# A down projection as seven products over pairs of row blocks, its operands' sums made earlier, its results added by accumulating transfers

## The chip, the cores and the metric

The kernel runs on one NeuronCore of a Trainium2 chip. The core has five engines with instruction queues of their own: TensorE (PE in the profile, with PEld for its weight loads), VectorE (DVE), ScalarE (ACT), GpSimd (POOL) and SyncE (SP), which here does nothing but issue transfers. Each queue runs in order, and queues wait for each other through semaphores. The metric is the device time of one launch in microseconds (us), the median of several runs.

## What is computed

One step of a hybrid encoder layer (a state space branch and a differential attention branch, then a convolutional feed-forward part) on 1088 tokens: 1024 of a prompt and 64 of running streams. The change lies in the last part of it:

```python
D_MODEL, D_FF, FFN_CONV = 1024, 2816, 3
    x = x + mix @ p['w_out']
    h = _rmsnorm(x, p['norm_ffn_w']) @ p['w_up']          # 1024 -> 2 * 2816
    ha, hb = jnp.split(h, 2, axis=-1)
    hc, ffn_new = _causal_dwconv(ffn_past, ha, p['ffn_conv_w'], p['ffn_conv_b'])
    x = x + (jax.nn.silu(hc) * hb) @ p['w_down']          # 2816 -> 1024
    return x, k, v, ssm_new, conv_new, ffn_new
```

## The kernel before

Activations are kept transposed: features on the 128 partitions, the 1088 tokens along the free axis. Everything is float32; a product is made of operands split into a high and a low half of the type fp32r (`hi` is ScalarE's rounded copy, `lo` is VectorE's difference), and three matmuls stand for one: hi*hi, hi*lo, lo*hi. A *split* below is this pair of instructions, the cast on ScalarE and the subtraction on VectorE.

The last two stages are the *way up* (`w_up`) and the *way down* (`w_down`).

**The way up** (`pair`, lines 970 to 1041 of the kernel before) takes 22 steps, here called pairs. One pair makes two row blocks of 128 features, block `f` of `ha` and block `f` of `hb`, over all tokens by a seven-product scheme of the Strassen-Winograd kind: the weights of the two blocks are cut in quarters (K halves by row blocks), the activations in quarters (K halves by token halves), and seven products of sums of quarters replace eight. Token quarters are 272 wide (`QW`), `s` is 0 or 1 for the two quarters of a half, and `p` counts the seven parts. One `(p, s)` is a *pile*: 4 tiles of K by 3 terms, 12 matmuls of 128x128 by 272 into a PSUM bank. So a pair is 14 piles, 168 matmuls. Seven banks go round; `a`, `b`, `c`, `d` are the accumulations of a pair, and `a`, `b`, `c` are read out once (an *evacuation*) and then added to further: p = 0 and 2 share `a`, p = 1 and 3 share `b`, p = 4 and 6 share `c`. So a pile of p = 6 can begin only when the evacuation of p = 4, same `s`, is done.

The right operands, `B[part, s]`, are made once ahead of the way up and live in units of SBUF (`home`). The left operands (`left_parts`, line 907) are made anew for each pair, one pair ahead: two transfers of the weights, four sums on GpSimd (lines 917, 918, 928, 935) and seven splits (lines 841, 842). When a pair's results are out, `gate` runs the convolution (two instructions on ScalarE and two on VectorE, line 1003, for each token half), GpSimd multiplies (line 1009) and SP stores the block to `h_sc` in DRAM (line 1010). The work for the second token half of a pair ends in the next pair.

**The way down** (lines 1080 to 1101) is a plain product. `hidden_row` reads a block of 128 rows of `h_sc` back (tile `hr`) and splits it into the units that the way up has left. The 22 blocks of K come in three groups of 8, 6 and 8 (`DOWN`). For each group and each of 8 blocks of output rows, the weights are loaded and split, then for token pieces of 384, 384 and 320 the running sum is loaded from DRAM (`xa`), a product of 3 times 8 (or 6) matmuls is made, VectorE adds the PSUM bank to `xa` (line 1097) and SP stores it (line 1098). The running sum goes through `x1_sc`, `x2_sc` and `x3_sc` to the output `yT`.

The order of each queue is set at build time by a list scheduler that goes by program order, priorities and its own timeline; it is the same in every run.

Of the kernel before, what the change touches and what calls it, by code (L numbers as in the profile page):

```python
# [17 lines left out]
P = 128  # L18
# [14 lines left out]
DOWN = (8, 6, 8)  # L33
# [42 lines left out]
def hybrid_layer(ctx: ExitStack, tc: tile.TileContext, xT, prm, cst, rope, wvd, win, wbs, wba, wout, wup, wdn,  # L76
# [773 lines left out]
    def output(m, quarters):  # L850
# [3 lines left out]
        for q in quarters:  # L854
# [10 lines left out]
            load(out=x1_sc[P * m : P * (m + 1), cs], in_=x)  # L865
# [42 lines left out]
    def left_parts(f):  # L908

        a = []  # L910
        for r in range(2):
            w = wp.tile([P, WMAX], F32, name="w_f", tag="w_f", bufs=2)
            load(out=w[:, :1024], in_=wup[f + r * FT])
            a += [w[:, :512], w[:, 512:1024]]
        q11, q12, q21, q22 = a
        s1, s2 = (row("fs", n)[:, :512] for n in ("ws1", "ws2"))
# [3 lines left out]
        def own(src):  # L920
            hi, lo = (row("fa", n, R32)[:, :512] for n in ("wh", "wl"))
            split(hi, lo, src)
            return hi, lo
# [6 lines left out]
        t = [wp.tile([P, WMAX], R32, name=n, tag=n, bufs=2) for n in ("w_hi", "w_lo")]  # L930
        for i, src in enumerate((s1, q22)):
            hi, lo = (x[:, 512 * i : 512 * i + 512] for x in t)
            split(hi, lo, src)
            yield hi, lo
        G.tensor_tensor(out=s2, in0=q12, in1=s2, op=ALU.subtract)
        hi, lo = (wp.tile([P, WMAX], R32, name=n, tag=n, bufs=2)[:, :512] for n in ("w_hi", "w_lo"))
        split(hi, lo, s2)
        yield hi, lo

# [16 lines left out]
    left = {0: list(left_parts(0))}  # L956
    coming = left_parts(1)
# [8 lines left out]
    def hidden_row(r):  # L966

        name, s = PARTS[r % 14 // 2], r % 2
        hi, lo = (unit(*at) for at in home[name, s])
        for j in range(2):  # L970
            t = couple(row("fb", "hr"))
            load(out=t, in_=h_sc[P * r : P * (r + 1), 2 * QW * j : 2 * QW * (j + 1)].rearrange("p (a t) -> p a t", a=2))
            split(hi[:, 2 * j : 2 * j + 2], lo[:, 2 * j : 2 * j + 2], t)
        return [u.rearrange("p a t -> p (a t)") for u in (hi, lo)]

    def pair(f):
# [6 lines left out]
        banks = {}  # L983

        def pile(key, p, s, start):
            if start:
                banks[key, s] = acc(QW)
            ps, w, b = banks[key, s], left[f][p], B[PARTS[p], s]
            for k in range(4):
                c = slice(P * k, P * (k + 1))  # L990
                for i, (x, y) in enumerate(((0, 0), (0, 1), (1, 0))):
                    PE.matmul(ps, w[x][:, c], b[y][:, k], start=start and k == i == 0, stop=k == 3 and i == 2,  # L992
                              skip_group_check=not start)
            return ps
# [48 lines left out]
    def begun(f):  # L1043
        u = pair(f)
        next(u)
        return u

    def more_left(f):
        x = next(coming, None)
        if x is not None:  # L1050
            left.setdefault(f, []).append(x)

    hid = []
# [16 lines left out]
    for f in range(1, FT):  # L1070
        coming = left_parts(f + 1) if f + 1 < FT else iter(())
        u = pairs[1] if f == 1 else begun(f)
        for p, s in rest[1] if f == 1 else [(p, s) for p in range(7) for s in range(2)]:
            u.send((p, s))
            if s == 1:
                more_left(f + 1)
                if f + 1 == FT and p < 4:
                    hid += [hidden_row(len(hid) + i) for i in range(2)]
        if f + 1 < FT:
            left.setdefault(f + 1, []).extend(coming)  # L1080
        del left[f]
    load(out=ffn, in_=ffn_o)


    k0, path = 0, (x1_sc, x2_sc, x3_sc, yT)
    for g, n in enumerate(DOWN):
# [121 lines left out]
```

## Time and profile before

| | |
|---|---|
| time, median of 3 runs | 2528.1 us (2526.99 to 2531.24) |
| span of the profiled execution, first to last instruction | 2526.9 us |
| TensorE busy | 2463.0 us, 97% of the span |
| VectorE, ScalarE, GpSimd busy | 60%, 45%, 21% |
| way up, steady part (21 pairs) | 1819.1 to 2240.2 us |
| last pair of the way up | 2240.2 to 2261.3 us |
| way down | 2261.3 us to the end |

The profile has no time of its own for the profiled execution beside its span; the median of the runs lies 1.2 us above that span. TensorE's busy time is a sum over stages, so what a change of one stage is worth is read in the windows of that stage. Columns of a window row are busy time and number of instructions of PE, PEld, DVE, ACT and POOL, the granted clock, the busy share of the transfer engines and what they moved. In a row of the timeline stand the start, the duration, the engine, the line and operation, and in brackets the idle time before it with what ended it. In a row of instruction groups stand the count, the busy time and the mean duration of one, then the idle time of the engine just before them.

### The profile page before, as it was taken

The page shows a single profiled execution, that of the slowest core. Times are in us where ns is not written, and L with a number is a line of the kernel's source. Part 1 is how long each engine was busy: PE and PEld are TensorE (multiplying, and loading weights), DVE is VectorE, ACT ScalarE, POOL GpSimd, SP SyncE. Part 2 cuts the span into 40 slices and gives each one's busy share as a digit, 9 for nine tenths or more (in the row PEclk, how much of TensorE's full clock was granted, in tenths as well). Part 3 has the DMA queues.
Part 4 walks back from the last instruction along what each step waited for, and adds up shares of the span by engine and source line. Part 5 has one row for each costly group of instructions (what it writes and reads, how often), then busy time and mean ns, then how long its engine had stood idle before and what let it go on. Part 6 is the DMA issues. An engine that isn't in the chain of part 4 may idle for free.

```text
span 2526.9 us, 43448 instructions
## 1 busy us (share of the span) xinstructions
PE 2463.0 (97%) x16646; PEld 2385.1 (94%) x16646; DVE 1507.9 (60%) x2597; ACT 1130.1 (45%) x2426; POOL 522.8 (21%) x584
## 2 busy tenths in 40 slices
PE   8999999999999999999999998999699999999999
PEld 8999999999999999998889898998699999999999
DVE  7326255855787677447667764645876666673422
ACT  6234343644666455357655654225443333341200
POOL 3000000100111001014333230014465555530000
PEclk9999999999999999999999999999799999999999
DMA  5217258545354344255697735663122222256553
GB/s 164 77 55 272 77 202 261 153 143 158 108 150 138 112 144 118 87 198 177 204 350 233 231 126 201 189 203 109 39 82 78 77 77 78 76 193 211 174 159 112
DMA packets 248336, 378.75 MB, mean 150 GB/s; under 512 B 31776, under 2 KB 188320, under 8 KB 248000
## 3 DMA queue, kind: packets, MB, share of 16 engines
q1 hardware_dynamic: 248128, 375.97, 46.6%
q8 instruction: 131, 2.15, 0.4%
q14 instruction: 77, 0.63, 0.1%
HBM read 254.58 MB, written 121.30 MB: 149 GB/s over the span
## 4 chain that ended last, share of the span: by engine, by line
PE 71%; DMA 4%; DVE 3%; ACT 2%; issue 1%; SPq 1%; POOL 0%; ACTq 0%; DVEq 0%; POOLq 0%
PE mx L992 12%; PE mm L149 10%; PE mm L151 10%; PE mm L150 10%; PE mm L992 5%; PE mx L151 4%; PE mx L149 4%; PE mx L150 4%; PE po L583 3%; PE sc L536 1%; PE sc L535 1%; PE pt L564 1%; PE yi L698 1%; PE ye L704 1%; DMA bc<-a_sc 1%; PE stp L710 1%
## 5 line engine op out<-in xcount | busy, mean ns | idle before, releaser
L149 PE MATMUL mm<-xn_hi,w_hi 128*128 128x384 f32 (+1 forms) x1416 | 469.8, 332 | 0.9 <-DVE zr L431 0.9
L151 PE MATMUL mm<-xn_hi,w_lo 128*128 128x384 f32 (+1 forms) x1416 | 467.7, 330 | 0.4 <-DVE w_lo L143 0.4
L150 PE MATMUL mm<-xn_lo,w_hi 128*128 128x384 f32 (+1 forms) x1416 | 466.5, 329 | 0.0
L142 ACT CAST w_hi<-w_f 128x1024 fp32r<-128x1024 f32 (+2 forms) x144 | 149.3, 1037 | 308.1 <-PE mx L150 162.2
L149 PEld LDWEIGHTS mm<-xn_hi,w_hi 128*128 128x128 f32 x1416 | 266.2, 188 | 5.3 <-issue 2.0
L151 PEld LDWEIGHTS mm<-xn_hi,w_lo 128*128 128x128 f32 x1416 | 266.1, 188 | 2.9 <-issue 0.8
L150 PEld LDWEIGHTS mm<-xn_lo,w_hi 128*128 128x128 f32 x1416 | 266.2, 188 | 1.8 <-issue 0.6
L143 DVE TENSOR_TENSOR w_lo<-w_f,w_hi 128x1024 fp32r<-128x1024 f32 (+2 forms) x144 | 181.2, 1259 | 133.4 <-ACT w_hi L142 133.0
L149 PE MATMUL mm<-b_hi,w_hi 128*128 128x384 f32 (+1 forms) x448 | 148.2, 332 | 7.6 <-DVE b_g L193 4.4
L151 PE MATMUL mm<-b_hi,w_lo 128*128 128x384 f32 (+1 forms) x448 | 147.0, 328 | 0.0
L150 PE MATMUL mm<-b_lo,w_hi 128*128 128x384 f32 (+1 forms) x448 | 146.9, 328 | 0.0
L992 PE MATMUL mx<-n,wh 128*128 128x272 f32 x752 | 143.4, 289 | 1.4 <-ACT wh L841 1.4
L992 PE MATMUL mx<-m,w_hi 128*128 128x272 f32 x752 | 142.7, 288 | 0.0
L460 DVE SCALAR_TENSOR_TENSOR cc<-pre,par,cc 128x384 f32<-128x384 f32 (+1 forms) x216 | 126.6, 586 | 23.8 <-ACT cc L458 18.7
L549 ACT ACTIVATE p_t<-sc,mx 128x1024 f32<-128x1024 f32 (+5 forms) x144 | 106.1, 739 | 74.6 <-DVE mx L540 37.1
L992 PEld LDWEIGHTS mx<-n,wh 128*128 128x128 f32 x752 | 118.3, 189 | 1.7 <-ACT wh L841 1.7
L992 PEld LDWEIGHTS mx<-m,w_hi 128*128 128x128 f32 x752 | 118.1, 188 | 0.0
L1009 POOL TENSOR_TENSOR hb<-hb,cc 128x544 f32<-128x544 f32 (+2 forms) x66 | 88.4, 1353 | 115.1 <-ACT w_hi L841 95.0
L151 PE MATMUL mx<-m,w_lo 128*128 128x272 f32 (+2 forms) x366 | 111.9, 307 | 0.0
L150 PE MATMUL mx<-m,w_hi 128*128 128x272 f32 (+2 forms) x366 | 111.9, 306 | 0.0
L149 PE MATMUL mx<-m,w_hi 128*128 128x272 f32 (+2 forms) x366 | 111.8, 306 | 0.0
L992 PE MATMUL mx<-m,w_lo 128*128 128x272 f32 x376 | 108.4, 288 | 0.0
(339 smaller groups left out, 6595.4 us busy)
## 6 DMA issues: line engine op xcount, KB each, us to landing
w_f<-in_win_dram SPq DMA_DIRECT2D x76, 512.0 KB, 3.8
w_f<-in_wup_dram SPq DMA_DIRECT2D x44, 512.0 KB, 3.5
bc<-a_sc SPq DMA_DIRECT2D x32, 512.0 KB, 6.1
h_sc<-hb SPq DMA_DIRECT2D x44, 272.0 KB, 2.1
hr<-h_sc SPq DMA_DIRECT2D x44, 272.0 KB, 5.2
x_sc<-cc SPq DMA_DIRECT2D x48, 192.0 KB, 2.2
xa<-x_sc SPq DMA_DIRECT2D x48, 192.0 KB, 2.5
kh_t<-k_st SPq DMA_DIRECT2D x32, 272.0 KB, 7.5
```

What stands on the lines that cost most here:

```text
L142: S.copy(hi, w)
L143: V.tensor_tensor(out=lo, in0=w, in1=hi, op=ALU.subtract)
L149: PE.matmul(ps, a_hi, b_hi, start=i == 0, stop=False)
L150: PE.matmul(ps, a_hi, b_lo, start=False, stop=False)
L151: PE.matmul(ps, a_lo, b_hi, start=False, stop=i == n - 1)
L460: V.scalar_tensor_tensor(cc[:, :m], pre[:, i : i + m], cw(i), cc[:, :m], ALU.mult, ALU.add)
L535: PE.matmul(ps[:n, a : a + b], lhs, r_hi, start=True, stop=False)
L536: PE.matmul(ps[:n, a : a + b], lhs, r_lo, start=False, stop=True)
L549: act(p_t[:n, :nk], sc[c][:n, :nk], AF.Exp, bias=mx[:n, c : c + 1], accum_out=dst)
L583: PE.matmul(po[:n, :P], a_t[b // 4][:kw, b % 4 * P : b % 4 * P + n], rhs, start=b == 0, stop=b == nb - 1)
L992: PE.matmul(ps, w[x][:, c], b[y][:, k], start=start and k == i == 0, stop=k == 3 and i == 2, skip_group_check=not start)
L1009: G.tensor_tensor(out=hb[h][:, o : o + n], in0=hb[h][:, o : o + n], in1=cc[:, d : d + n], op=ALU.mult)
```

## The change

The way down becomes 12 further steps of the kind of the way up. K is in groups of 8, 8 and 6 row blocks; a group is cut in two halves of 4, 4 and 3 tiles (even and odd row blocks). Within a group, four steps (`pair_down`) each make two blocks of 128 output rows over all tokens by the seven products: 14 piles of 12 matmuls in the first two groups, of 9 in the third. Its left operands go through `left_parts` with blocks of `w_down`, packed anew on the host.

The right operands need sums of quarters of the hidden rows. They are made during the way up: in every second pair, from pair 2 on, `hidden_sums` reads the two row blocks stored last (four transfers into `g` tiles of the ring `fb`), makes the four sums t1 to t4 on GpSimd, and stores them to a new scratch `t_sc` (four transfers). In the last step ahead of each group, `hidden_part` runs after each part p: it loads the part's operand from `h_sc` or `t_sc` (four `hr` tiles a part, 28 a group) into the units that this p has just set free, and splits them; of the four subtractions one goes to GpSimd.

The running sum in DRAM goes. The way up's input `x1` is stored to the output `yT` itself, and each of the four quarter results of a step (128 x 544) is added to `yT` by a transfer that GpSimd issues with an accumulating write, 48 of them in all. There are no `xa` tiles.

```diff
-DOWN = (8, 6, 8)
+DOWN = (8, 8, 6)
...
-    x1_sc, x2_sc, x3_sc = (scratch(n, [D, T]) for n in ("x1_sc", "x2_sc", "x3_sc"))
     h_sc = scratch("h_sc", [DFF, T])
+    t_sc = scratch("t_sc", [4 * DFF // 2, T // 2])
...
-            load(out=x1_sc[P * m : P * (m + 1), cs], in_=x)
+            load(out=yT[P * m : P * (m + 1), cs], in_=x)
...
+    DOWN_AT = [sum(DOWN[:g]) for g in range(len(DOWN))]
+    work = [(None, f) for f in range(FT)] + [(g, j) for g in range(len(DOWN)) for j in range(4)]
+
+    def left_of(i):
+        g, f = work[i]
+        if g is None:
+            return left_parts([wup[f], wup[f + FT]])
+        n, o = P * DOWN[g], 1024 * DOWN_AT[g]
+        return left_parts([wdn[:, o + n * m : o + n * (m + 1)] for m in (2 * f, 2 * f + 1)])
...
+    def hidden_sums(i):
+
+        b11, b12, b21, b22 = (row("fb", n)[:, :HALF] for n in ("g11", "g12", "g21", "g22"))
+        e = row("fb", "ge")[:, :HALF]
+        for u, (x, y) in enumerate(((b11, b12), (b21, b22))):
+            for v, t in enumerate((x, y)):
+                load(out=t, in_=h3[:, 2 * i + u, HALF * v : HALF * (v + 1)])
+        G.tensor_tensor(out=e, in0=b12, in1=b11, op=ALU.subtract)
+        G.tensor_tensor(out=b12, in0=b22, in1=b12, op=ALU.subtract)
+        G.tensor_tensor(out=b11, in0=b22, in1=e, op=ALU.subtract)
+        G.tensor_tensor(out=b21, in0=b21, in1=b11, op=ALU.subtract)
+        for n, t in zip(KIND, (e, b11, b12, b21)):
+            load(out=t3[:, KIND.index(n), i], in_=t)
+
+    def hidden_part(g, name):
+
+        i0, nk = DOWN_AT[g] // 2, DOWN[g] // 2
+        for s in range(2):
+            hi, lo = B[name, s] = [unit(*at) for at in home[name, s]]
+            for j in range(0, nk, 2):
+                n = min(2, nk - j)
+                t = couple(row("fb", "hr"))[:, :n]
...
+                load(out=t, in_=src)
+                S.copy(hi[:, j : j + n], t)
+                (G if s and j else V).tensor_tensor(out=lo[:, j : j + n], in0=t, in1=hi[:, j : j + n], op=ALU.subtract)
...
+    def pair_down(g, j):
...
+        def put(m, h, t):
+            G.dma_start(out=yT[P * m : P * (m + 1), HALF * h : HALF * (h + 1)], in_=t, accum_op=ALU.add)
...
+            if p == 0:
+                S.copy(u1[:, s], pile("a", p, s, True))
+            elif p == 1:
+                V.tensor_tensor(out=u2[:, s], in0=pile("b", p, s, True), in1=u1[:, s], op=ALU.add)
+            elif p == 2:
+                S.copy(c[p][:, qs], pile("a", p, s, False))
+            elif p == 3:
+                V.tensor_tensor(out=u1[:, s], in0=pile("b", p, s, False), in1=u1[:, s], op=ALU.add)
+            elif p == 4:
+                V.tensor_tensor(out=c[p][:, qs], in0=pile("c", p, s, True), in1=u1[:, s], op=ALU.add)
...
+            if s == 1 and p in (2, 4, 5, 6):
+                m, h = {2: (0, 0), 4: (1, 1), 5: (1, 0), 6: (0, 1)}[p]
+                put(2 * j + m, h, c[p])
...
+    for i, (g, f) in enumerate(work[1:], 1):
+        coming = left_of(i + 1) if i + 1 < len(work) else iter(())
+        u = pairs[1] if i == 1 else begun(i)
+        last = i + 1 < len(work) and work[i + 1][0] not in (g, None)
+        for p, s in rest[1] if i == 1 else [(p, s) for p in range(7) for s in range(2)]:
+            u.send((p, s))
+            if s == 1:
+                more_left(i + 1)
+                if last:
+                    hidden_part(work[i + 1][0], PARTS[p])
+                if p == 3 and i < FT + 2 and i % 2 == 0:
+                    hidden_sums(i // 2 - 1)
```

Up to the way up the queues read as before, row for row, but for the target of the `x1` stores. In the way up, TensorE, VectorE and ScalarE keep their order as well; what is new there stands on GpSimd and SP. Three places of the build's order follow.

GpSimd in one pair of the way up, before: behind the sums of the weights (`ws`, `w_f`) and the two small copies comes the multiplication for the first token half.

```order
L1009 TENSOR_TENSOR hb<-hb,cc 128x480
L1009 TENSOR_TENSOR hb<-hb,cc 128x64
L935 TENSOR_TENSOR ws_19395<-w_f,ws_19395 128x512
L1023 COPY pre<-pre 128x2
L982 COPY pre<-par 128x2
L1009 TENSOR_TENSOR hb<-hb,cc 128x544
L1038 COPY con<-pre 128x2
```

The same place after, in every second pair (the line numbers are those of the changed kernel).

```order
L1051 TENSOR_TENSOR hb<-hb,cc 128x480
L1051 TENSOR_TENSOR hb<-hb,cc 128x64
L936 TENSOR_TENSOR ws_19394<-w_f,ws_19394 128x512
L1065 COPY pre<-pre 128x2
L1035 COPY pre<-par 128x2
L989 TENSOR_TENSOR ge<-g_19501,g_19500 128x544
L990 TENSOR_TENSOR g_19501<-g_19503,g_19501 128x544
L991 TENSOR_TENSOR g_19500<-g_19503,ge 128x544
L992 TENSOR_TENSOR g_19502<-g_19502,g_19500 128x544
L1051 TENSOR_TENSOR hb<-hb,cc 128x544
L1080 COPY con<-pre 128x2
```

The four sums stand between the small copies and the multiplication for the first token half.

VectorE in the last pair of the way up, before: low halves of hidden rows (`n<-hr,n`, `m<-hr,m`, units) between the evacuations `u<-mx` of p = 1 and p = 3 and the convolution (`cc`).

```order
L1019 TENSOR_TENSOR u_24167<-mx,u_24166 128x272
L842 TENSOR_TENSOR n_24209<-hr,n_24208 128x544
L842 TENSOR_TENSOR n_24247<-hr,n_24246 128x544 x2
L842 TENSOR_TENSOR m_24257<-hr,m_24256 128x544
L1026 TENSOR_TENSOR u_24166<-mx,u_24166 128x272
L1003 SCALAR_TENSOR_TENSOR cc<-pre,par,cc 128x544
L842 TENSOR_TENSOR m_24257<-hr,m_24256 128x544
```

The same place after.

```order
L1061 TENSOR_TENSOR u_24335<-mx,u_24334 128x272
L1011 TENSOR_TENSOR n_24389<-hr,n_24388 128x544
L842 TENSOR_TENSOR wl<-ws_24371,wh 128x512
L1011 TENSOR_TENSOR n_24431<-hr,n_24430 128x544 x2
L1011 TENSOR_TENSOR m_24441<-hr,m_24440 128x544
L842 TENSOR_TENSOR wl<-w_f,wh 128x512
L1068 TENSOR_TENSOR u_24334<-mx,u_24334 128x272
L1045 SCALAR_TENSOR_TENSOR cc<-pre,par,cc 128x544
```

Between the same two evacuations now stand the low halves of the next step's weights (`wl`) as well; before, no seven-product step followed this pair.

GpSimd at the same time, after (before, it has only the multiplications and small copies of that pair there): from the last weights' sum of pair 21 to the first accumulating transfer.

```order
L936 TENSOR_TENSOR ws_24371<-w_f,ws_24371 128x512
L1065 COPY pre<-pre 128x2
L1011 TENSOR_TENSOR m_24441<-hr,m_24440 128x544
L1011 TENSOR_TENSOR n_24497<-hr,n_24496 128x544
L1051 TENSOR_TENSOR hb<-hb,cc 128x544
L1011 TENSOR_TENSOR m_24548<-hr,m_24547 128x544
```

```order
L918 TENSOR_TENSOR ws_24758<-w_f 128x512
L1051 TENSOR_TENSOR hb<-hb,cc 128x480
L1051 TENSOR_TENSOR hb<-hb,cc 128x64
L919 TENSOR_TENSOR ws_24759<-ws_24758,w_f 128x512
L929 TENSOR_TENSOR w_f<-w_f 128x512
L1011 TENSOR_TENSOR m_24652<-hr,m_24651 128x544
L1092 DMA out_dram<-down 128x544
L1011 TENSOR_TENSOR m_24714<-hr,m_24713 128x544
```

The subtractions of hidden parts, the sums for the weights of the step after next and the first accumulating transfer now stand in one queue.

More of the change, by code (lines that the diff above doesn't have):

```diff
@@ L929, in left_parts @@
         yield own(q21)
-        t = [wp.tile([P, WMAX], R32, name=n, tag=n, bufs=2) for n in ("w_hi", "w_lo")]
+        t = [wp.tile([P, WMAX], R32, name=name, tag=name, bufs=2) for name in ("w_hi", "w_lo")]
         for i, src in enumerate((s1, q22)):
-            hi, lo = (x[:, 512 * i : 512 * i + 512] for x in t)
+            hi, lo = (x[:, 512 * i : 512 * i + n] for x in t)
             split(hi, lo, src)
@@ L964, in hybrid_layer @@
     ffn_o = tri[:, : 4 * FT].rearrange("p (f c) -> p f c", c=4)
[L966 to L974, printed above, removed]
+    HALF = 2 * QW
@@ L982, in pair @@
         G.tensor_copy(pre[1][:, 482:484], par[:, O_FS + 2 * f : O_FS + 2 * f + 2])
[L983 to L994, printed above, removed]
+        pile = piles(f, 4)
         def gate(h):
```

99 lines of the change are left out of this document (56 added, 43 removed).

## Prediction, made before the changed kernel was run

> **What bounds the kernel now.** I read the head of the page first, then windows around the two stages, then single rows at their borders.
>
> ```profile
> span 2526.9 us, 43448 instructions
> PE 2463.0 (97%) x16646; PEld 2385.1 (94%) x16646; DVE 1507.9 (60%) x2597; ACT 1130.1 (45%) x2426; POOL 522.8 (21%) x584
> ```
>
> TensorE is busy nearly everywhere, so a stage is worth its matmuls unless another engine makes it wait. The windows of the stages that the change touches (way up, a steady pair, last pair, way down), and then the rows at the borders of the way down:
>
> ```profile
> 1819.10:2261.30 442.20, 442.20 (x3528) 442.20 (x3527) 307.44 (x475) 181.52 (x323) 230.30 (x246) 1.00 0.27 90
> 1861.04:1882.11 21.07, 21.07 (x170) 21.07 (x169) 14.58 (x23) 8.28 (x15) 10.98 (x12) 1.00 0.23 79
> 2240.20:2261.30 21.10, 21.10 (x170) 21.10 (x169) 16.74 (x31) 14.55 (x25) 3.74 (x6) 1.00 0.95 333
> 2261.20:2520.00 258.80, 258.11 (x1564) 257.85 (x1563) 86.60 (x130) 41.77 (x56) 4.21 (x5) 1.00 0.53 170
> ...
> 2261.34 0.33 PE L149 MATMUL mm<-n,w_hi 128*128 128x384 f32 x1
> ...
> 2523.28 0.31 PE L151 MATMUL mx<-m,w_lo 128*128 128x320 f32 x1
> ...
> 2523.62 0.49 DVE L1097 TENSOR_TENSOR xa<-xa,mx 128x320 f32<-128x320 f32 x1 [2.96 <-PE mx L151]
> ```
>
> TensorE never stops in either stage, at a granted clock of 1.00. VectorE has 14.6 of 21.1 us of work in a steady pair, GpSimd 11.0. In the way down both are nearly free.
>
> **TensorE's part.** The way up runs 3528 matmuls of 272 columns in 442.2 us, 125.3 ns each (the 288 ns of the group rows overlap). The way down before is 8 row blocks x 3 token pieces x 22 tiles x 3 terms = 1584 matmuls, from 2261.3 to 2523.6, 262.3 us or 165.6 ns each. After, it is four steps of 168, four more of 168 and four of 126: 1848 matmuls of 272 columns. I take the 125.3 ns of the way up, where the same instructions stand: 231.6 us. Gain 30.7 us, if nothing makes TensorE wait. Nothing else of the removed work was on the path: the `xa` loads and stores and the VectorE additions ran beside TensorE (258.1 of 258.8 us busy), all but the last, which is in the tail.
>
> **The port that VectorE and GpSimd share.** What the new steps add is on these two engines, and the rows show that they get in each other's way:
>
> ```profile
> 2216.91 0.69 DVE L842 TENSOR_TENSOR w_lo<-ws,w_hi 128x512 fp32r<-128x512 f32 x1
> 2217.52 1.85 DVE L842 TENSOR_TENSOR w_lo<-w_f,w_hi 128x512 fp32r<-128x512 f32 x1
> ...
> 2216.96 1.85 POOL L1009 TENSOR_TENSOR hb<-hb,cc 128x544 f32<-128x544 f32 x1 [4.66 <-ACT w_hi L841]
> ...
> 2186.82 0.69 DVE L842 TENSOR_TENSOR wl<-w_f,wh 128x512 fp32r<-128x512 f32 x1 [1.23 <-ACT wh L841]
> ...
> 2186.89 1.77 POOL L935 TENSOR_TENSOR ws<-w_f,ws 128x512 f32<-128x512 f32 x1
> ...
> L928 POOL TENSOR_TENSOR w_f<-w_f 128x512 f32<-128x512 f32 x19 | 24.6, 1294 | 0.0
> L1030 DVE TENSOR_TENSOR hb<-mx,u 128x272 f32<-128x272 f32 x29 | 12.8, 442 | 29.7 <-PE mx L992 29.0 <-issue 0.7
> ```
>
> The split of 0.69 us takes 1.85 when GpSimd is in the middle of a multiplication: it ends 0.6 us behind GpSimd's end at 2218.81. The other way round, GpSimd's sum of 1.29 us takes 1.77 when VectorE began first. The evacuations, which read PSUM and one SBUF tile, keep their 0.44 us. So the sums of both engines with two SBUF inputs add up. Net prices: a split of 512 columns 0.61 (2216.91 to 2217.52), and, from the rows below, one of 544 0.66 (three in 1.99), `cc` 0.80 (two in 1.61), GpSimd's 480 and 64 together 1.48; GpSimd's 512 is 1.29, so its 544 is an estimated 1.37 by columns.
>
> ```profile
> 2274.70 1.99 DVE L842 TENSOR_TENSOR m<-hr,m 128x544 fp32r<-128x544 f32 x3
> ...
> 2242.18 1.61 DVE L1003 SCALAR_TENSOR_TENSOR cc<-pre,par,cc 128x546 f32<-128x546 f32 x2 [0.38 <-ACT cc L1001]
> ...
> 2244.57 1.48 POOL L1009 TENSOR_TENSOR hb<-hb,cc 128x480 f32<-128x480 f32 x2 [2.60 <-ACT cc L1004]
> ```
>
> [...]
>
> **First border, way up to group 0.** Of the 28 hidden tiles a group, VectorE subtracts 21 and GpSimd 7. All stand in pair 21 and the step behind it. From the `cc` at 2242.18, 2 us into pair 21, to the last subtraction of the last part (b22), GpSimd's order holds: the sums for two steps less the last of the second (7 x 1.29), 7 x 1.37, the two second-half multiplications (2 x 1.48) and the one of 544 (1.37), 23.0 us. VectorE's holds 21 x 0.66, eight weight splits (8 x 0.61) and six `cc` (4.8): 23.6 us. Together 46.6 us. TensorE needs b22 at p = 6 of step 22, 18 us into it (14 piles in 21.07 us, 1.5 each), so 39 us after pair 21 begins, 37 behind that `cc`. It comes some 10 us late, and already in pair 21 the evacuation of p = 4, which p = 6 needs 4.5 us later, stands behind 11 of the hidden tiles. Bounds: VectorE alone with both pairs' evacuations (23.6 + 20 x 0.44 = 32.4) fits into 37: 0. If the evacuations too come in a row with the rest: 46.6 + 8.8 - 37 = 18. [...]
>
> **Second and third border.** There is no convolution: GpSimd 4 x 1.29 + 7 x 1.37 = 14.8, VectorE 13.9 + 4.9 = 18.8, 33.6 in the 36 us from 3 us into step 25 to the use of b22 in step 26. That fits at the end, not on the way: the evacuation of p = 4 has 11 subtractions, 4 weight splits, 4 evacuations and, at most, four weight sums and four subtractions of GpSimd ahead (7.3 + 2.4 + 1.8 + 10.7 = 22.2 from 1.5 on), while p = 6 wants it at 18: up to 5.7 us late, or 0 if GpSimd's come in later. I take 4. The third border has three tiles instead of four, and I take 1 (0 to 3). ScalarE's 28 casts a border, at 0.65 each (row below), are 18 us in 42, where it has 8.3 in a steady pair: covered.
>
> ```profile
> L841 ACT CAST m<-hr 128x544 fp32r<-128x544 f32 x18 | 11.4, 647 | 7.2 <-DMA hr<-h_sc 6.9
> ...
> h_sc<-hb SPq DMA_DIRECT2D x44, 272.0 KB, 2.1
> hr<-h_sc SPq DMA_DIRECT2D x44, 272.0 KB, 5.2
> ...
> out_dram<-xa SPq DMA_DIRECT2D x16, 192.0 KB, 2.4
> ```
>
> Transfers there: 28 x 272 KB, 7.8 MB, are 23 us at the 333 GB/s of the last pair's window, within 39 us. They too take the place of others: on SP the weights of step 23 stand behind 23 of the 28 loads.
>
> **The sums in the way up.** Four on GpSimd, 4 x 1.37 = 5.5 us in ten pairs (the eleventh is in step 22), where GpSimd waits:
>
> ```profile
> L1009 POOL TENSOR_TENSOR hb<-hb,cc 128x544 f32<-128x544 f32 x20 | 37.0, 1850 | 96.9 <-ACT w_hi L841 95.0 <-DVE hb L1030 1.9
> ...
> 2218.84 0.32 SPq L1010 DMA_DIRECT2D h_sc<-hb  x1
> 2219.39 0.33 SPq L913 DMA_DIRECT2D w_f<-in_wup_dram  x1
> ```
>
> 96.9 us of idle time ahead of 20 multiplications is 4.8 a pair, just where the sums are put, so they push GpSimd back by about 1 us. SP gets four loads and four stores; the second weight load of the next pair stands behind the stores, hence behind the sums. VectorE loses up to 5.5 us of port in 6.5 us of idle time a pair; the evacuation of p = 3 comes later, but p = 6 waits only for p = 4. I take 0; the bounds are 0 and 1 us for each of the ten pairs.
>
> **GpSimd's 48 accumulating transfers.** No row shows one. Issuing costs between SP's 0.33 us and one GpSimd sum, 1.29; four a step, 1.3 to 5.2 us beside 5.2 of sums in 21, are covered in steps without hidden parts. At the borders the transfer for p = 2 waits for its evacuation with GpSimd's subtractions behind it; these are needed a step later. Their landing is on the path only at the end. **Tail:** before, from the last matmul (2523.6) to the end of the span, 3.3 us: 0.49 of VectorE and a store of 2.4 and some. After, 0.44, an issue, and a transfer of 272 KB that reads and writes: between a store alone (2.1) and a load and a store (5.2 + 2.1), with issue 2.9 to 9.0 us, -0.4 to +5.7. Nearer to a store with something added, I take +2. [...]
>
> **Sum.** -30.7 + 10 + 4 + 1 + 0 + 2 = -13.7 us. The profiled span is 2526.9, the median of the runs 1.2 above it; I set the sum against the median: 2528.1 - 13.7 = 2514.4.
>
> **Rivals.** [...] *The sums slow the way up* (slower): they take GpSimd and with it the port just when VectorE has the splits and evacuations at a pair's end; p = 3 and p = 4 of the next pair slip past the 4.5 us that TensorE has before p = 6. Place: ten pairs. Decides from 1.4 us a pair (13.7 / 10); at 2.7, half of the sums, it costs 27 and gives 2541. For it: the port has 4 x 1.29 + 1.37 + 1.48 of GpSimd and 7 x 0.61 + 4 x 0.80 of VectorE, 15.5 us in 21.1, and 21.0 with the sums, full. Against: the next pair has 5.6 free, and nothing of it is due within the pair. *The gain is eaten at the borders*: the first at its 18, the second at 6, the third at 3, tail and issue 5: 2529, no change. *The scheme doesn't save*: 1848 matmuls for 1584; excluded by the 125.3 against 165.6 ns in rows of the same kernel.
>
> **How the numbers follow.** Forecast 0.52 (its own range 2506 to 2522), all hidden 0.16, eaten 0.14, slower by the way up 0.13, another stall that I don't see (GpSimd's queue behind a transfer) 0.05, beyond 2533. A measurement of this kernel tells from no change about 0.2%, 5 us. Faster: 0.52 + 0.16 and a little of eaten, 0.70; within: 0.11; slower: 0.19. The range 2499 to 2534 takes in the bounds of the borders and leaves out the slow cases' far end and the gain without any wait.
>
> **What would show it.** Right: windows of the way down with 125 ns a matmul between borders; TensorE idle behind VectorE or ScalarE in the last pair of the way up and in step 22, some 10 us, with splits of 1.3 us and more; less in steps 25 and 26; the way up still 21.1 us a pair. Wrong: pairs of the way up longer than 21.1 us in every second one; borders without idle time; TensorE waiting for weights behind SP's `hr` loads; an end more than 6 us behind the last matmul.

## The result, and the profile after

The changed kernel takes 2529.3 us (median of 20 runs, 2523.2 to 2535.0), the kernel before, beside it on the same chip, 2529.4 us (20 runs, 2526.8 to 2531.9). The ratio is 1.0000 with a 95% interval of 0.9993 to 1.0007: no change. The profiled execution of the changed kernel has a span of 2525.8 us. What follows shows that the 30 us of matmuls were saved, and where they went.

The page of the changed kernel (span, and busy time of each engine):

```profile
span 2525.8 us, 44652 instructions
PE 2440.0 (97%) x16910; PEld 2358.9 (93%) x16910; DVE 1612.5 (64%) x2724; ACT 1184.8 (47%) x2574; POOL 723.2 (29%) x745
```

TensorE is busy 23 us less than before, the span is the same. The windows of the changed kernel (columns as before: PE, PEld, DVE, ACT, POOL, granted clock, transfers): the steady way up, the stretch of its last pair, and the way down (the borders are those of the kernel before; the changed kernel's execution was 1.6 us ahead by then).

```profile
1819.10:2240.20 421.10, 421.10 (x3360) 421.10 (x3359) 308.08 (x445) 165.84 (x298) 280.34 (x280) 1.00 0.38 130
2240.20:2261.30 21.10, 18.16 (x132) 17.72 (x130) 16.53 (x20) 11.40 (x22) 14.73 (x12) 0.92 0.86 278
2261.30:2526.00 264.70, 241.46 (x1872) 239.36 (x1872) 171.99 (x267) 100.12 (x204) 135.94 (x120) 0.97 0.73 166
```

In the way up TensorE never stops, although GpSimd has the sums of the hidden rows there as well. In the next stretch it has 132 matmul records where it had 170 before, and the mean granted clock of this stretch and of the way down is below 1.00. What TensorE waited for (the view of waits, engine PE, from 1819 us on; us in total, times, longest), largest first:

```profile
PE mx L1023 <- DVE down L1109: 5.3, 2, 4.9
PE mm L1023 <- DVE down L1109: 4.2, 1, 4.2
PE mx L1023 <- DVE u L1061: 2.4, 1, 2.4
PE mx L1023 <- ACT u L1101: 2.3, 2, 1.4
PE mx L1023 <- DVE u L1103: 2.2, 3, 1.1
PE mx L1023 <- DVE hb L1070: 1.7, 1, 1.7
```

These ten waits are 18.1 us. All of them are for an evacuation (p = 4 of a step of the way down on L1109, of pair 21 on L1070; p = 0 on L1101, p = 1 on L1061 and L1103), none is directly for a tile of hidden rows or for weights. (The wait on L1061 goes back to late hidden rows all the same: that evacuation stood in VectorE's queue behind subtractions whose tiles had not come; the rows are shown with e14_two_late below.) The longest one, in step 22, with VectorE's, GpSimd's and TensorE's rows of the timeline:

```profile
2285.47 1.85 DVE L842 TENSOR_TENSOR wl<-ws,wh 128x512 fp32r<-128x512 f32 x1
2287.59 4.56 DVE L842 TENSOR_TENSOR wl<-w_f,wh 128x512 fp32r<-128x512 f32 x1
2292.07 0.43 DVE L1109 TENSOR_TENSOR down<-mx,u 128x272 f32<-128x272 f32 x1
...
2284.93 1.84 POOL L1011 TENSOR_TENSOR m<-hr,m 128x544 fp32r<-128x544 f32 x1
2286.71 1.01 POOL L1092 DMA_DIRECT2D out_dram<-down  x1
2287.45 1.65 POOL L1011 TENSOR_TENSOR m<-hr,m 128x544 fp32r<-128x544 f32 x1
2288.76 1.56 POOL L936 TENSOR_TENSOR ws<-w_f,ws 128x512 f32<-128x512 f32 x1
2289.98 1.62 POOL L989 TENSOR_TENSOR ge<-g,g 128x544 f32<-128x544 f32 x1
...
2292.65 0.79 PE L1023 MATMUL mx<-m,w_hi 128*128 128x272 f32 x2 [4.93 <-DVE down L1109]
```

VectorE's split of the weights began 0.14 us after GpSimd's subtraction and ended 0.55 us after the end of the third GpSimd operation in a row (2291.60): 4.56 us for work of 0.61. The evacuation stood behind it, and TensorE behind the evacuation. The split just ahead of it, at 2285.47, had waited for one GpSimd operation only: it ended 0.55 us after that one's end at 2286.77.

The timeline rows and windows after the three stalls of over 2 us, for the clock:

```profile
2362.24 0.43 PE L1023 MATMUL mm<-m,w_lo 128*128 128x272 f32 x1
...
2367.56 0.29 PE L1023 MATMUL mx<-n,wl 128*128 128x272 f32 x1
...
2251.53:2257.50 5.97, 5.97 (x36) 5.97 (x37) 5.97 (x6) 5.97 (x13) 5.48 (x4) 0.73 0.78 245
2292.65:2298.00 5.35, 5.35 (x32) 5.35 (x33) 5.35 (x6) 0.62 (x1) 4.24 (x4) 0.72 0.89 202
2361.62:2367.23 5.61, 5.61 (x25) 5.61 (x26) 5.61 (x10) 3.70 (x7) 3.20 (x3) 0.50 0.98 279
```

The single matmuls behind the third stall take 0.43 us at first and 0.29 later. TensorE comes back at a lower granted clock: in the last of these windows it is 0.50, 25 matmuls in 5.61 us where 45 fit at 125 ns. The time lost is the length times the missing share of the clock: 5.97 x 0.27 + 5.35 x 0.28 + 5.61 x 0.50 = 5.9 us. Behind the shorter waits, of 1.67 us and less, the clock stayed at 1.00. The first of the three stalls, with 0.73 behind it, was 2.37 us long.

The end. Before, 3.3 us lay between the last matmul and the end of the span. After (last evacuation and last transfer, from the timeline, and the row of the transfers):

```profile
2517.97 0.44 DVE L1113 TENSOR_TENSOR down<-mx,u 128x272 f32<-128x272 f32 x1 [0.69 <-PE mx L1023]
2518.70 0.86 POOL L1092 DMA_DIRECT2D out_dram<-down  x1 [1.40 <-DVE down L1113]
...
out_dram<-down POOLq DMA_DIRECT2D x48, 272.0 KB, 4.9
```

The last matmul ends at 2517.9, the span at 2525.8: 7.9 us, 7.1 of them behind the start of the last issue.

### The profile page after: what moved, and what is told of

It reads as the page before. It is cut to its first block, busy times and chain, and to the rows that moved or that the text cites. A ratio compares the mean times of both kernels' runs of the same rounds, so it can differ in the third digit from the quotient of the medians.

```text
span 2525.8 us, 44652 instructions
## 1 busy us (share of the span) xinstructions
PE 2440.0 (97%) x16910; PEld 2358.9 (93%) x16910; DVE 1612.5 (64%) x2724; ACT 1184.8 (47%) x2574; POOL 723.2 (29%) x745
## 5 line engine op out<-in xcount | busy, mean ns | idle before, releaser
L143 DVE TENSOR_TENSOR w_lo<-w_f,w_hi 128x1024 fp32r<-128x1024 f32 (+1 forms) x120 | 152.7, 1273 | 127.6 <-ACT w_hi L142 127.1
L1023 PE MATMUL mx<-n,wh 128*128 128x272 f32 x1156 | 222.0, 290 | 6.2 <-ACT u L1101 2.3
L1023 PE MATMUL mx<-m,w_hi 128*128 128x272 f32 x1114 | 214.4, 290 | 7.0 <-DVE down L1109 5.3
L1023 PEld LDWEIGHTS mx<-n,wh 128*128 128x128 f32 x1156 | 182.8, 190 | 7.3 <-ACT u L1101 2.8
L142 ACT CAST w_hi<-w_f 128x1024 fp32r<-128x1024 f32 (+1 forms) x120 | 125.7, 1049 | 131.2 <-PE mm L150 74.5
L1023 PEld LDWEIGHTS mx<-m,w_hi 128*128 128x128 f32 x1114 | 177.3, 191 | 7.6 <-issue 5.1
L1023 PE MATMUL mx<-n,wl 128*128 128x272 f32 x578 | 167.2, 290 | 0.0
L1023 PE MATMUL mx<-m,w_lo 128*128 128x272 f32 x557 | 161.6, 290 | 0.0
L460 DVE SCALAR_TENSOR_TENSOR cc<-pre,par,cc 128x384 f32<-128x384 f32 (+1 forms) x216 | 126.5, 586 | 23.5 <-ACT cc L458 18.4
L841 ACT CAST w_hi<-ws 128x512 fp32r<-128x512 f32 (+1 forms) x68 | 41.4, 608 | 169.6 <-PE mx L1023 122.9
L842 DVE TENSOR_TENSOR wl<-w_f,wh 128x512 fp32r<-128x512 f32 (+1 forms) x102 | 94.7, 928 | 30.3 <-ACT wh L841 29.6
```

The lines of the kernel that those rows point to most:

```text
L142: S.copy(hi, w)
L143: V.tensor_tensor(out=lo, in0=w, in1=hi, op=ALU.subtract)
L460: V.scalar_tensor_tensor(cc[:, :m], pre[:, i : i + m], cw(i), cc[:, :m], ALU.mult, ALU.add)
L841: S.copy(hi, src)
L842: V.tensor_tensor(out=lo, in0=src, in1=hi, op=ALU.subtract)
L1023: PE.matmul(ps, w[x][:, c], b[y][:, k], start=start and k == t == 0, stop=k == nk - 1 and t == 2, skip_group_check=not start)
```

## The experiments

Each kernel was timed beside runs of the kernel before. The stages ahead of the way down differ by some us from one execution to the next, so the table has a second measure, from one trace each: from the start of ScalarE's first evacuation in pair 21 to the end of the span (in the changed kernel 2525.8 - 2240.49 = 285.3; in the kernel before 284.9). Being from one trace each, it scatters: e5_late_sums, where GpSimd's queue stands in the same order as in the changed kernel, is 2.6 us away from it.

| kernel | median us (runs) | ratio to before, 95% | pair 21 to the end, us |
|---|---|---|---|
| changed kernel | 2529.3 (20) | 1.0000 (0.9993 to 1.0007) | 285.3 |
| e1_no_parts | 2505.8 (4) | 0.9908 (0.9896 to 0.9921) | 258.3 |
| e4_no_low | 2508.0 (4) | 0.9920 (0.9906 to 0.9934) | 262.8 |
| e2_low_on_v | 2518.2 (6) | 0.9954 (0.9940 to 0.9968) | 273.0 |
| e10_low_on_g | 2564.2 (4) | 1.0144 (1.0128 to 1.0160) | 316.2 |
| e5_late_sums | 2530.2 (11) | 1.0008 (0.9999 to 1.0017) | 282.7 |
| e3_plain_store | 2519.5 (7) | 0.9966 (0.9954 to 0.9978) | 274.1 |
| e7_tail_by_sp | 2513.9 (5) | 0.9946 (0.9933 to 0.9960) | 268.4 |
| e6_left_on_v | 2515.5 (5) | 0.9951 (0.9938 to 0.9963) | 269.8 |
| e14_two_late | 2521.3 (9) | 0.9954 (0.9936 to 0.9971) | 268.1 |
| e15_two_late_left_v | 2515.8 (5) | 0.9938 (0.9924 to 0.9953) | 269.4 |

My theory after the result: the matmuls are saved in full, and VectorE's and GpSimd's work on the hidden rows at the borders makes evacuations late, since the two engines hold each other up (above, a split of 0.61 us took 4.56); *the port* in what follows is a name for this alone. Rivals: the loads of the hidden rows are late; the accumulating transfers are in the way; the scheme saves less than the way up promised.

**No work on the hidden rows.** The operands of the way down are neither loaded nor split; TensorE multiplies what lies in the units.

```diff
             if s == 1:
                 more_left(i + 1)
-                if last:
-                    hidden_part(work[i + 1][0], PARTS[p])
```

> Leaves out hidden_part in all three borders: no hidden tiles are loaded or split, and the way down multiplies by the operands that the way up left in the units. The way up, its sums, the weights, the evacuations and the accumulating transfers stay. If the borders are the whole of what ate the gain (TensorE ran 25 us longer there than its matmuls take), 2529.3 - 25 = 2504 us, with TensorE without idle time up to the end. If TensorE is held by something else in the way down (weights, GpSimd's transfers), 2515 or more, and idle time stays in the trace.

Measured: 2505.8 us, 23.5 below the changed kernel by the medians, 27.0 by the traces. The window of its way down (step 22 to the last matmul):

```profile
2268.30:2500.30 232.00, 231.96 (x1848) 231.73 (x1847) 112.61 (x204) 60.96 (x128) 103.64 (x99) 1.00 0.58 112
```

1848 matmuls in 232.0 us, 125.5 ns each, at a clock of 1.00 and without idle time. So the saving of the scheme is there whole (262.3 - 232.0 = 30.3 us), and the borders cost 23.5 to 27 us. The rival "saves less" falls.

**Casts without subtractions.** Loads and ScalarE's casts stay; the low halves are left out, the products use what lies in their units.

```diff
-            hi, lo = B[name, s] = [unit(*at) for at in home[name, s]]
+            hi = unit(*home[name, s][0])
+            B[name, s] = [hi, B[name, s][1]]
...
-                (G if s and j else V).tensor_tensor(out=lo[:, j : j + n], in0=t, in1=hi[:, j : j + n], op=ALU.subtract)
```

> Hidden tiles are loaded and cast as before, but no low half is made (the units keep those of the way up): the 28 subtractions of a border go, its transfers and ScalarE's casts stay. If the time of VectorE and GpSimd on their common port makes the border, 2506 to 2512 us, next to the kernel without hidden parts. If late transfers or ScalarE's queue make it, most of the idle time of TensorE stays: 2520 or more.

Measured: 2508.0 us, 21.3 below the changed kernel by the medians and 22.5 by the traces. TensorE's remaining waits:

```profile
PE mx L1023 <- DVE hb L1070: 1.5, 1, 1.5
PE mx L1023 <- ACT u L1101: 1.5, 2, 1.0
```

With all the loads and casts still there, 83% (22.5 of 27.0) to 91% (21.3 of 23.5) of the borders' cost is gone. It hangs on the subtractions: the transfers and ScalarE's casts account by themselves for no more than the rest. This run doesn't part the port from VectorE's own 21 subtractions a border, nor from late tiles, for which only a subtraction makes VectorE wait; the next two runs move work between the two engines instead.

**All subtractions on VectorE.** One engine does the same work, 21 of the 84 subtractions move to VectorE, so it has more to do, and GpSimd less.

```diff
-                (G if s and j else V).tensor_tensor(out=lo[:, j : j + n], in0=t, in1=hi[:, j : j + n], op=ALU.subtract)
+                V.tensor_tensor(out=lo[:, j : j + n], in0=t, in1=hi[:, j : j + n], op=ALU.subtract)
```

> All low halves of the hidden tiles on VectorE, none on GpSimd. Port theory (VectorE waits for GpSimd's whole instructions, GpSimd's cost twice VectorE's): a border's common time falls by 7 x (1.37 - 0.66) = 5 us, and VectorE waits less in between: 2520 us (2515 to 2525). Theory that VectorE itself has too much to do at the borders: 7 x 0.66 = 4.6 us more for it at each, 2533 or more. Theory of late tiles (transfers): no change, 2529.

Measured: 2518.2 us, faster than before by 0.46%. The same place of step 22 in its timeline:

```profile
2288.04 1.65 DVE L842 TENSOR_TENSOR wl<-w_f,wh 128x512 fp32r<-128x512 f32 x1
2289.61 0.77 DVE L1109 TENSOR_TENSOR down<-mx,u 128x272 f32<-128x272 f32 x2
...
2291.01 0.67 DVE L842 TENSOR_TENSOR w_lo<-ws,w_hi 128x512 fp32r<-128x512 f32 x1
...
2287.88 1.26 POOL L936 TENSOR_TENSOR ws<-w_f,ws 128x512 f32<-128x512 f32 x1
...
2290.86 1.78 POOL L1092 DMA_DIRECT2D out_dram<-down  x2
...
2290.10 0.52 PE L1023 MATMUL mx<-m,w_hi 128*128 128x272 f32 x2 [2.05 <-DVE down L1109]
```

The split waits for one GpSimd sum now, 1.65 us instead of 4.56, and the stall is 2.05 instead of 4.93. In the second border the stall of 4.20 is down to 0.50, and two of 1.68 and 1.17 follow in step 26, for ScalarE's evacuation of p = 0. In these rows two issues alone don't hold VectorE up: the split at 2291.01 takes 0.67 us in the middle of them.

**All subtractions on GpSimd**, the opposite, as a check that it isn't any shift of work that helps.

```diff
-                (G if s and j else V).tensor_tensor(out=lo[:, j : j + n], in0=t, in1=hi[:, j : j + n], op=ALU.subtract)
+                G.tensor_tensor(out=lo[:, j : j + n], in0=t, in1=hi[:, j : j + n], op=ALU.subtract)
```

> All 28 low halves of a border on GpSimd, none on VectorE; nothing is left out. Port theory: GpSimd needs 21 x 1.37 = 28.8 us more at the first and second border, VectorE 13.9 less, so the common time grows by 15 us at each and some 11 at the third: 2529 + 41 = 2570 (2550 to 2590). Theory that VectorE has too much to do of its own: it has 14 us less at each border, 2515 or faster.

Measured: 2564.2 us, 34.9 above the changed kernel, near the 2570 of the port theory. VectorE and GpSimd ahead of the longest wait, and the three longest waits of TensorE:

```profile
2370.45 11.73 DVE L842 TENSOR_TENSOR w_lo<-w_f,w_hi 128x512 fp32r<-128x512 f32 x1
2382.10 0.43 DVE L1113 TENSOR_TENSOR down<-mm,u 128x272 f32<-128x272 f32 x1
...
2369.92 0.88 POOL L1092 DMA_DIRECT2D out_dram<-down  x1
2370.53 5.50 POOL L1011 TENSOR_TENSOR n<-hr,n 128x544 fp32r<-128x544 f32 x4
...
2378.09 3.53 POOL L1011 TENSOR_TENSOR m<-hr,m 128x544 fp32r<-128x544 f32 x2
...
PE mm L1023 <- DVE down L1113: 10.7, 1, 10.7
PE mx L1023 <- ACT m L1010: 9.4, 1, 9.4
PE mx L1023 <- DVE down L1113: 6.6, 1, 6.6
```

Two of the three longest waits are for an evacuation on VectorE, which has 63 instructions fewer than in the changed kernel. Ahead of the longest one a split of 0.61 us took 11.73, until GpSimd's work, seven operations and two issues, was over at 2381.62; the evacuation stood behind it. The third of the waits is for a tile of hidden rows itself.

**One sum less at the first border, by program order.** The sums of the last two row blocks, whose first one (`ge`) is the third GpSimd operation of the stall shown above, move in the program from step 22 to step 24.

```diff
-                if p == 3 and i < FT + 2 and i % 2 == 0:
-                    hidden_sums(i // 2 - 1)
+                if p == 3 and (i < FT and i % 2 == 0 or i == FT + 2):
+                    hidden_sums(min(i // 2 - 1, FT // 2 - 1))
```

> The last of the eleven sets of sums (rows 20 and 21), which is made in step 22, in the middle of the first border, moves to step 24; nothing is left out. In the trace a weight split in step 22 took 4.56 us behind three instructions of GpSimd in a row, one of them such a sum, and the evacuation behind it held TensorE for 4.9 us. Port theory: that stall shrinks to under 1 us, and its share of lower granted clock goes too: 2523 us (2521 to 2526). Otherwise no change, 2529.

Measured: 2530.2 us, ratio 1.0008 (0.9999 to 1.0017), not the gain that I expected. The stall stays as long as it was, and so does what stood ahead of it:

```profile
2287.79 4.56 DVE L842 TENSOR_TENSOR wl<-w_f,wh 128x512 fp32r<-128x512 f32 x1
...
2290.17 1.61 POOL L989 TENSOR_TENSOR ge<-g,g 128x544 f32<-128x544 f32 x1
...
2292.84 0.79 PE L1023 MATMUL mx<-m,w_hi 128*128 128x272 f32 x2 [4.93 <-DVE down L1109]
```

The list scheduler put the sum back where it was: `ge` is still the third operation of the stall, and from 2241 us on GpSimd's 132 instructions stand in the same order in both traces. So this run can't say what the sum is worth, and whether the stall needs it stays open. It serves as a second execution of the same order on GpSimd. The stalls of 4.93 and 4.20 us come again to the hundredth, while the first one of pair 21, 2.37 us in the changed kernel, isn't there, and the one for `hb` is 3.87 instead of 1.67. Behind the two long stalls the clock is 0.61 and 0.74, where the changed kernel has 0.72 and 0.50.

**Plain stores by SP.** The results are stored instead of added: the 48 transfers are SP's, and adding to the running sum is left out.

```diff
-            G.dma_start(out=yT[P * m : P * (m + 1), HALF * h : HALF * (h + 1)], in_=t, accum_op=ALU.add)
+            load(out=yT[P * m : P * (m + 1), HALF * h : HALF * (h + 1)], in_=t)
```

> The results of the way down are stored to the output by SP as they are; leaves out adding them to what stands there (the input x1 and the groups before). Measures what the 48 accumulating transfers cost. If they cost only at the end (in the profile 7.9 us from the last matmul to the end of the span, 3.3 before the change): 4.5 us less, 2525. If their issue on GpSimd (0.86 us each) also holds the port at the borders: another 3 to 6 us less, 2519 to 2522.

Measured: 2519.5 us, 9.9 below the changed kernel (11.2 by the traces). Its transfers:

```profile
out_dram<-down SPq DMA_DIRECT2D x48, 272.0 KB, 2.7
```

The end is 3.6 us behind the last matmul instead of 7.9: 4.3 us. The other 5.6 (medians) to 6.9 us (traces) lie ahead of the end; the interval of the ratio leaves 1 to 7 us for them. TensorE's waits come to 13.0 us instead of 18.1: the one of 4.93 is 1.87, the one of 4.20 is 3.73, and the one for `hb` in pair 21, which differs as much between executions of one order, is 3.85 instead of 1.67. One thing is gone altogether: in this trace no split waits for more than one GpSimd operation, and the longest takes 1.9 us. In the changed kernel the two splits that waited for several (4.56 and 4.12 us) both began while GpSimd issued an accumulating transfer; here GpSimd issues none. Each issue also takes 0.86 us of GpSimd's queue; what each of the two is worth isn't told apart.

**The last results without the accumulating transfer.** All subtractions on VectorE, and besides, in the last step, the running sum for the last two quarters (p = 5, 6) is loaded ahead, added to `u1` and `u2` on VectorE, and SP stores the results. Nothing is left out.

```diff
+            if end and s == 0 and p in (0, 1):
+                h = 1 - p
+                y[h] = row("fb", "ysum")[:, :HALF]
+                load(out=y[h], in_=yT[P * (2 * j + 1 - h) : P * (2 * j + 2 - h), HALF * h : HALF * (h + 1)])
+            if end and p == 2:
+                V.tensor_tensor(out=u2[:, s], in0=u2[:, s], in1=y[1][:, qs], op=ALU.add)
+            if end and p == 5:
+                V.tensor_tensor(out=u1[:, s], in0=u1[:, s], in1=y[0][:, qs], op=ALU.add)
...
-                put(2 * j + m, h, c[p])
+                if end and p in (5, 6):
+                    load(out=yT[P * (2 * j + m) : P * (2 * j + m + 1), HALF * h : HALF * (h + 1)], in_=c[p])
+                else:
+                    put(2 * j + m, h, c[p])
```

> All low halves on VectorE, and in the last step the results of p = 5 and p = 6 not by accumulating transfers: what stands in the output is loaded ahead by SP, added to u1 and u2 on VectorE before they are needed, and the results are stored by SP. Nothing is left out. The end shrinks from 7.9 to 3.5 us behind the last matmul: 2518.2 - 4.4 = 2514 (2512 to 2516). If the end of the span waits for something else, no change, 2518.

Measured: 2513.9 us, 0.9946 (0.9933 to 0.9960) of before. Its span and last evacuation:

```profile
span 2510.5 us, 44660 instructions
...
2506.92 0.44 DVE L1123 TENSOR_TENSOR down<-mx,u 128x272 f32<-128x272 f32 x1 [0.69 <-PE mx L1023]
```

3.6 us behind the last matmul, the 4.3 us that the transfer cost. This kernel computes the whole and beats both: 14.5 us less than the kernel before, 2528.4 beside it.

**The weights' sums on VectorE too.** All subtractions on VectorE, and besides the four sums of the weights for each step of the way down.

```diff
-    def left_parts(blocks):
+    def left_parts(blocks, eng=G):
...
-        G.tensor_tensor(out=s1, in0=q21, in1=q22, op=ALU.add)
+        eng.tensor_tensor(out=s1, in0=q21, in1=q22, op=ALU.add)
...
-        return left_parts([wdn[:, o + n * m : o + n * (m + 1)] for m in (2 * f, 2 * f + 1)])
+        return left_parts([wdn[:, o + n * m : o + n * (m + 1)] for m in (2 * f, 2 * f + 1)], V)
```

> All low halves of the hidden tiles on VectorE, and the four sums for the left operands of each step of the way down as well (28 + 4 instructions a border and step, none on GpSimd). By the port alone the common time of the first border falls from 41.6 to 36.8 us and that of the second to 28: 2512. If VectorE's own time is the next limit (with 8.8 us of evacuations it has 41 of 37 us at the first border and 37 of 36 at the second): no better than the kernel with only the low halves on VectorE, 2518 (2515 to 2522).

Measured: 2515.5 us, at the lower edge of what the second expectation allows; the intervals of this kernel and of e2_low_on_v (0.9938 to 0.9963 and 0.9940 to 0.9968) overlap, so the gain of 2.7 us over it by the medians is not shown.

**Two sums later.** e7_tail_by_sp, and two of the three sets of sums that only the third group needs (row blocks 18 to 21; the expectation's 16 to 19 is a slip) move in the program to steps 23 and 24, so that the transfers of the first of them leave SP's queue ahead of the first loads of hidden rows. In the trace the first operations of these sets begin at 2285.5 and 2296.8 us, where the changed kernel has 2233.7 and 2290.0.

```diff
-                if p == 3 and i < FT + 2 and i % 2 == 0:
-                    hidden_sums(i // 2 - 1)
+                if p == 3 and (i < FT - 2 and i % 2 == 0 or i in (FT + 1, FT + 2)):
+                    hidden_sums(i // 2 - 1 if i < FT else i - FT + 8)
```

> As e7_tail_by_sp, and besides that the sums of row blocks 16 to 19 and 20 to 21 of the hidden rows, which only the third group of K needs, move out of the pairs in front of the border: the last two calls stand in steps 23 and 24. With them their four stores and four loads leave SP's queue ahead of the first loads of hidden rows. If the first stall in pair 21 (1.2 us in e7, 2.4 in the changed kernel) is loads of hidden rows that come late behind those transfers, it vanishes with what follows from it: 2510 to 2512 us. If these transfers were never on the path, no change from e7: 2514.

Measured: 2521.3 us, 2510.6 to 2526.7, neither of the two expectations. ScalarE's first casts of hidden rows in the changed kernel, by the timeline:

```profile
2246.27 0.65 ACT L1010 CAST n<-hr 128x544 fp32r<-128x544 f32 x1 [2.30 <-DMA hr<-h_sc]
2249.38 0.65 ACT L1010 CAST n<-hr 128x544 fp32r<-128x544 f32 x1 [2.46 <-DMA hr<-h_sc]
```

And in this kernel:

```profile
2248.54 1.42 ACT L1010 CAST n<-hr 128x544 fp32r<-128x544 f32 x2 [0.57 <-DMA hr<-h_sc]
2250.12 0.65 ACT L1010 CAST n<-hr 128x544 fp32r<-128x544 f32 x1 [0.15 <-DMA hr<-h_sc]
```

The first tiles come with less of a wait (0.57 and 0.15 us), and the first stall of pair 21 is gone; e5_late_sums, where nothing was moved ahead of it, lacks that stall too, so its absence in one trace isn't shown to come from the edit. From pair 21 to the end the trace has 268.1 us against 268.4 in e7_tail_by_sp, no difference given the scatter. Of its nine runs, three are below 2512.3 and five at 2521.3 or more; only one, of 2515.1, has a trace, and what lengthens the others stays open.

**Both together.** e14_two_late with the weights' sums of e6_left_on_v on VectorE.

> e14_two_late with the four weight sums of each step of the way down on VectorE instead of GpSimd, as e6 did to e2, where it was worth 2.7 us. If what is left at the borders is GpSimd in VectorE's way, it gives the same here, 2508 to 2510 us; if VectorE's own time is the bound by now, these 0.61 to 0.7 us each on VectorE cost as much as they save: 2511 to 2514.

Measured: 2515.8 us, a little over the worse of the two expectations. Its VectorE and TensorE in step 24:

```profile
2325.14 0.69 DVE L918 TENSOR_TENSOR ws<-w_f 128x512 f32<-128x512 f32 x1 [6.55 <-DMA w_f<-in_wdn_dram]
...
2327.07 0.43 DVE L1113 TENSOR_TENSOR u<-mx,u 128x272 f32<-128x272 f32 x1
...
2327.56 0.53 PE L1023 MATMUL mx<-m,wh 128*128 128x272 f32 x2 [4.10 <-DVE u L1113]
```

VectorE waits 6.55 us for the weights' transfer with an evacuation behind it in its queue, and TensorE loses 4.1 us. While the sums stood on GpSimd, no evacuation was queued behind them.

## Why the prediction was wrong, step by step

- **TensorE, -30.7 us: right.** e1_no_parts shows 1848 matmuls in 232.0 us (231.6 forecast), a gain of 30.3.
- **The sums in the way up, 0: right.** TensorE is busy for 421.10 of 421.10 us in the 20 steady pairs (3360 matmuls at 168 a pair; the table ahead of the prediction calls them 21), with GpSimd at 280 us of work. The rival that forecast a slower kernel from there, *the sums slow the way up*, is out.
- **The borders, 10 + 4 + 1 = 15 us: the step that failed.** These 15 us were waits alone. In the changed kernel the first border has 12.1 us of waits and 3.1 of lower clock (1.6 + 1.5), the second 4.2 and 2.8, the third 1.9: 18.1 us of waits and 5.9 of clock, 24.1 in all, and the difference to e1_no_parts is 23.5 to 27. The larger part of the miss is the clock, for which the sum had no term at all. Of the waits, the first (2.4, and 1.6 of clock behind it) comes in the main from late hidden rows and not from the port.
- **The waits, size and place.** That evacuations come late because VectorE and GpSimd hold each other up was forecast, and it is what the rows show for the long waits (4.93 and 4.20 us). For the second border the forecast held as it stood: VectorE works without a pause from 2341.9 us to the evacuation of p = 4 at 2361.14, and TensorE waits 4.2 us for it (4 forecast). For the first border the 10 us stood on the last tile, b22, coming late; no wait is for it. Choosing 10 between the bounds of 0 and 18 rested on my estimate that the two engines hold each other up wherever they meet; no run shows that as a rule. What the runs show in its place is 12.1 us, which came as six waits for evacuations, so that the near size is in part luck. Each price in the working was a wait for one operation of the other engine (a split of 0.61 at 1.85); the longest wait came from a split that waited for three, 4.56 us.
- **The tail, +2: too small, +4.6.** 7.9 us against 3.3. My bounds (-0.4 to +5.7) held it; I took the value near a plain store, and the transfer that adds takes 4.9 us to land, against 2.7 for the plain one in e3_plain_store.
- **The 48 transfers beside other work, 0: too small.** e3_plain_store gains 5.6 to 6.9 us ahead of the tail (1 to 7 by its interval). This is no further term of the sum, since it is part of the waits above. The prediction had put their issuing at nothing in steps without hidden parts, and at the borders it had let them wait without a price.
- **The sum.** -30.3 + 24.1 + 4.6 = -1.6 us, measured 0.0; the rest, some 2 us, may be idle time in pieces too short to be listed or the shift between executions, which isn't told apart. Against the forecast of -13.7 the clock is 5.9 us, the waits 3.1, the tail 2.6 and the matmuls 0.4. *The gain is eaten at the borders*, 2529 us at a chance of 0.14, is what came. *All hidden*, the borders at 0 and 2499 us at a chance of 0.16, did not: the borders cost 23.5 to 27 us.
- **The weights behind SP's loads, and late hidden rows.** No wait of TensorE is for weights. Late hidden rows, which I had put at nothing because 23 us of transfers fit into 39, do make the first stall (2.30 and 2.46 us of ScalarE's idle time, with VectorE's subtractions and the evacuation behind them). It isn't in every execution, and e14_two_late doesn't show that removing it gains anything.

That the two engines hold each other up agrees with e2_low_on_v (2518.2 us) and e10_low_on_g (2564.2 us) in direction. That a split can wait for three GpSimd operations (4.56 us), and in e10_low_on_g for seven (11.73 us), is more than I had reckoned with.

## What to carry to other kernels

When work is moved into the shadow of a saturated engine, ask not whether the sum of it fits in the time, but which short instruction, on whose end the saturated engine depends, stands in line behind it, and what the longest single wait there can be. With two engines that hold each other up, as VectorE and GpSimd do here (a split of 0.61 us took 1.85 beside one GpSimd operation and 4.56 beside three), look at which of them holds the short urgent instructions: here 0.46% came from giving VectorE more work and GpSimd less, and the opposite cost 1.4%. And give a stall of TensorE a second price at a lower clock, which here was a third of the waits (5.9 for 18.1 us).

## What the runs showed of the hardware that I had not expected

- VectorE mostly goes first between two GpSimd operations that follow each other. From 1819 us on, the changed kernel's trace has 68 places where a VectorE operation with two SBUF inputs waits as one GpSimd operation ends and the next begins within 0.1 us, and VectorE goes first; such waits end 0.3 to 0.6 us behind the first GpSimd operation. In 3 places it is passed over, by the splits of 4.56 us (twice) and 4.12 us. There GpSimd's rows overlap by 0.3 us and more (2287.45 + 1.65 against 2288.76), elsewhere by 0.11 at most, and each of these stretches opens with the issue of an accumulating transfer. e3_plain_store, without such issues, has 77 places and none where VectorE is passed over; e2_low_on_v, with the issues but fewer GpSimd operations behind them, has 61 and none either; e10_low_on_g has 23, all but one in such stretches. Why the issue brings this about is not shown.
- Issuing an accumulating transfer took 0.86 us of GpSimd's queue (the last one of the changed kernel, at 2518.70), and alone it didn't hold VectorE up: in e2_low_on_v a split in the middle of two issues took 0.67.
- A transfer of 272 KB that adds to DRAM landed in 4.9 us (changed kernel, 48 of them), a plain store of the same tile in 2.7 (e3_plain_store).
- The clock fell behind a stall of only 2.06 us, to 0.70, and not by the length of the stall alone. The windows behind stalls of 2.05 us in e2_low_on_v and 2.06 us in e7_tail_by_sp:

```profile
2290.10:2295.70 5.60, 5.60 (x44) 5.60 (x45) 4.66 (x9) 1.43 (x3) 4.60 (x5) 1.00 0.94 248
```

```profile
2288.80:2294.40 5.60, 5.60 (x32) 5.60 (x33) 3.22 (x8) 0.80 (x2) 4.47 (x5) 0.70 0.96 250
```

44 matmuls in one, 32 in the other, after nearly the same pause at the same place of the program. After pauses of 2.53 us in e2_low_on_v and 2.51 in e6_left_on_v the clock is 0.69 and 1.00. What tells them apart wasn't tried.
